# Five columns spread by repeated transposes, an opening in another order, and a last output chunk in two halves of 128 tokens

## The chip, the core and the metric

One core of a Trainium2 chip runs the whole kernel. Its engines work side by side, each in its own program order: TensorE (PE, with its weight loads shown apart as PEld), VectorE (DVE), ScalarE (ACT), GpSimd (POOL) and SyncE (SP), whose queue issues most DMAs; ACT issues some. They wait for each other by semaphores. The metric is the device time of one execution in microseconds, the median of several runs.

## The reference

Two layers over 512 tokens of width 1024, with a context of 256 tokens. Per layer, `h = rmsnorm(x) * (1 + s) + sh`, where shift and scale are columns of `silu(c) @ w_mod + b_mod`. Layer 0 mixes by chunked gMLP spatial gating and by neighbourhood attention (8 heads of 64, window 8 x 16, plus the context keys); layer 1 by a Conformer convolution (31 taps, LayerNorm, SiLU). Each is followed by a squared-ReLU MLP of width 4096. The output is the RMS-normed stream:

```
x = x + g1 * mixer(modulate(rmsnorm(x, g), sh1, s1))
x = x + g2 * (relu(modulate(rmsnorm(x, g'), sh2, s2) @ w1) ** 2 @ w2)
...
return rmsnorm(x, final_g)
```

## The kernel before

Activations lie with the model width on the 128 partitions (8 tiles of 128 x 512 tokens). Each product of 128 x 128 weights by 512 tokens is made of three matmuls in fp32r (`hi*hi`, `lo*hi`, `hi*lo`, lines 88 to 90 in `mm3`), with weights and activations split into a high and a low part: ACT copies the high part (L148 for weights), DVE or POOL subtracts it for the low part (L143). The order of every engine's instructions is written out by hand; nothing is rescheduled.

Statistics of a token are a column: after a matmul against ones with the tokens as stationary side, 128 tokens lie on the partitions. To use them on tiles that have tokens along the free axis, the column has to be repeated and turned. Before, this is a full fp32 matmul, the column broadcast to 128 columns as the stationary side and the identity as the moving side. This is done in five places:

- `deviations` (L441): four columns of the first RMS norm; `silu_rows` (L446): here the eight columns of `silu(c)` are first multiplied into diagonals on DVE (L434), and ones against a diagonal gives the repeated row.
- `weigh` (L963): for each of four pairs of heads, the reciprocals of the softmax sums of the pair's eight blocks, as matmuls of 64 columns each.
- `stats` (L1434): mean and reciprocal deviation of the convolution's LayerNorm, in two calls for each half of the tokens.
- `tail1` (L1581): the last RMS norm's factor for the second half of the tokens.

Opening. `mod_products(f)` makes a quarter of the first modulation in four steps: four matmuls (L457), four more and an ACT copy to `ms` (L462), four transposes (L466), and three small DVE operations that end in `gsA` (L471 to L474). The code between the steps orders the rest: `deviations`, `scaled` (DVE, L498), `silu_rows`, `W.piece` (L148 and L143 for a quarter of a weight tile), `first_operand` (ACT makes the high part of two tiles, L504; DVE the rest, L505, L506) and `first_products` (L493).

Attention. A loop takes the 16 units (pair of heads, quarter of the tokens) two at a time: `scores` for both (PE), `weigh` for the two before (PE, L955), `soften` (DVE L922, ACT exponent L926), and then seven steps n = 0 to 6, each with one `more(1)`: a piece of other work from `filling()` (projections, the spatial gate L790 to L869, and products), in whose staged parts ACT and DVE answer each other. At n = 2 and 3 `turn` transposes the exponents (L939) and ACT copies them (L941); with the last quarter of a pair it takes the reciprocal of the sums (L934). At n = 0, 2, 5 (from the seventh loop round on only at 5) `work(1)` runs one DVE job of the later modulations (L599). After the eighth round the last two `weigh` follow, and PE goes on with `more(100)`.

Tail. `tail1` computes the last 128 rows of the output for the second 256 tokens: matmuls, `evac` (DVE, L1073), square (ACT, L343), sums against ones (L1575), root (L1577), reciprocal (L1578), spread (L1581), copy (L1583), six products on DVE and two on POOL (L1586), four output DMAs on SP (L1588).

Of the kernel before, what the change touches and what calls it, by code (L numbers as in the profile page):

```python
# [17 lines left out]
P = 128  # L18
# [37 lines left out]
def body(ctx: ExitStack, tc: tile.TileContext, I: dict, out: bass.AP):  # L56
# [28 lines left out]


# [345 lines left out]
    dgs = [slot(s="dgc") for _ in range(2)]  # L432
    for k in range(KC):
        dve.tensor_scalar(dgs[k // 4][:, k % 4 * P : k % 4 * P + P], ident, sc[:, k, 0:1], None, op0=ALU.mult)  # L434
    r0 = slot(s="rstd")

    def deviations():

        ps = bank()
        for n in range(4):  # L440
            pe.matmul(ps[:, n * P : (n + 1) * P], dev[:, n : n + 1].to_broadcast([P, P]), ident, start=True, stop=True)  # L441
        act.copy(r0, ps)

    def silu_rows(i):
        ps = bank()
        pe.matmul(ps, ones, dgs[i], start=True, stop=True)  # L446
        return ps
# [52 lines left out]
    def first_operand(f):  # L500
        for k in (2 * f, 2 * f + 1):
            gs, sh = colA(0, k)
            hi, lo = h[k]
            act.activation(hi, x0[k], AF.Identity, scale=gs, bias=sh)  # L504
            dve.tensor_scalar(x0[k], x0[k], gs, sh, op0=ALU.mult, op1=ALU.add)  # L505
            dve.tensor_tensor(lo, x0[k], hi.bitcast(F32), op=ALU.subtract)  # L506
# [6 lines left out]
    next(pm)  # L513
    pbs = [silu_rows(0)]
# [4 lines left out]
    W.piece(0, 0)  # L519
# [371 lines left out]
    sm, pts, po, yb, tot = {}, {}, {}, {}, {}  # L891
# [38 lines left out]
    def turn(u):  # L930
        pts[u] = []
        p_, j = units[u]
        if j == 3:
            dve.reciprocal(tot[p_], tot[p_])  # L934
        for e in range(2):
            s = sm[u][e]
            pt = bank()
            for i in range(4):
                pe.transpose(pt[:, i * P : (i + 1) * P], s[:, i * P : (i + 1) * P], ident)  # L939
            t = blk(s="pt") if u % 2 else mp.tile([P, 512], F32, tag="pt", name=nm("pt"), bufs=2)  # L940
            act.copy(t, pt)  # L941
            pts[u].append(t)
        del sm[u]

    def weigh(u):
# [12 lines left out]
        if j == 3:  # L958

            pr = bank()  # L960
            for i in range(4):
                for e in range(2):
                    pe.matmul(pr[64 * e : 64 * e + 64, i * P : (i + 1) * P],  # L963
                              tot[p_][:, 4 * e + i : 4 * e + i + 1].to_broadcast([P, 64]), ident,
                              start=True, stop=True)
            rs = slot(s="rs")
            act.copy(rs, pr)
            b = ahalf("yb", p_)
            dve.tensor_tensor(tok(b), perm(po[p_]), perm(rs), op=ALU.mult)
            yb[p_] = b  # L970
# [47 lines left out]
    for u in range(0, NU, 2):  # L1018
# [7 lines left out]
        for n in range(7):  # L1026
# [3 lines left out]
            if n == 3:  # L1030
                turn(u + 1)
            if n in ((0, 2, 5) if u < 12 else (5,)):
# [38 lines left out]
    def residual(gate, ss):  # L1071
        def evac(m, ps, t0, t1):
            dve.scalar_tensor_tensor(x[:, m, t0:t1], ps, gate[:, m : m + 1], x[:, m, t0:t1],  # L1073
                                     op0=ALU.mult, op1=ALU.add)
            if ss is not None:
# [284 lines left out]
    def conv_module(h):  # L1360
# [69 lines left out]
        def stats(t0, n):  # L1430

            q, r, ps = stat[t0]
            for i in (2 * n, 2 * n + 1):
                pe.matmul(ps[:, i * P : (i + 1) * P], q[:, i : i + 1].to_broadcast([P, P]), ident,  # L1434
                          start=True, stop=True)
# [96 lines left out]
    def tail1(acts, ev, ss, ff, third):  # L1532
# [35 lines left out]
        seven = together([(7, v, P)], acts, ev, b0, b1)[0]  # L1568
        seven()
        gained((7,))  # L1570
        sq, ss.late = ss.late[0], None
        tot_ = bank()
        for n in range(2):
            for i, t in enumerate((ss.acc[:, b0:b1], sq)):
                pe.matmul(tot_[:, n : n + 1], t[:, n * P : n * P + P], ones[:, :1], start=i == 0, stop=i == 1)  # L1575
# [4 lines left out]
        for n in range(2):  # L1580
            pe.matmul(pr[:, n * P : n * P + P], q[:, n : n + 1].to_broadcast([P, P]), ident, start=True, stop=True)  # L1581
# [5 lines left out]
        for k0, k1 in ((0, 1), (1, 3), (3, 6), (6, 8)):  # L1587
            sync.dma_start(out[:, k0:k1, b0:b1], ob[:, k0:k1, :])  # L1588
# [87 lines left out]
```

## Time and profile before

| what | value |
|---|---|
| median of 3 runs | 1166.35 us (1165.97 to 1166.97) |
| the profiled execution's own time | 1164.55 us |
| its span, first to last instruction | 1162.8 us |
| PE busy, by the modelled ends of its matmuls | 1150.3 us |
| DVE, ACT, POOL busy | 724.8, 479.7, 153.0 us |
| HBM read, written | 152.52 MB, 2.10 MB |

Matmuls overlap in the pipeline, so PE's busy time hides short waits; the distance from one start to the next tells what a matmul costs. An fp32 matmul leaves two records, a transpose or an fp32r matmul one.

### The profile page before, as it was taken

The numbers are of one execution on the slowest core, as the hardware profiler recorded it, in microseconds if no ns is written. First come the engines' busy times: TensorE is split into PE (matmuls) and PEld (weight loads), VectorE is DVE, ScalarE is ACT, GpSimd is POOL, SyncE is SP. The second block draws the span as 40 slices with busy tenths as digits, with TensorE's granted clock in tenths as the row PEclk, the third lists the DMA queues.
The fourth block names the chain that finished last, engine by engine and source line by source line (L and its number), as shares of the span: only waits on it lengthen the run. The fifth ranks groups of instructions, "written<-read, shape, count | busy, mean of one in ns | idle before, by whom it ended". The sixth has DMA issues, their size and how long they took to land. (4 is left out here: it accounts for less than half of the span.)

```text
span 1162.8 us, 16541 instructions
## 1 busy us (share of the span) xinstructions
PE 1150.3 (99%) x6612; PEld 956.9 (82%) x6612; DVE 724.8 (62%) x1258; ACT 479.7 (41%) x955; POOL 153.0 (13%) x149
## 2 busy tenths in 40 slices
PE   9999999999999999999999999999999999999997
PEld 5788898889888888888889666699888888888887
DVE  4855786878665665666677879577643443443544
ACT  5564557446422422423246223575531331332423
POOL 0041234433000000000024110153100000000001
PEclk9999999999999999999999999999999999999998
DMA  9634543351565555555531444313232232232222
GB/s 370 247 125 134 167 149 110 121 192 62 205 236 181 188 210 181 191 207 181 203 123 56 145 126 125 98 37 110 73 109 100 82 109 102 79 109 78 105 73 73
DMA packets 32333, 161.91 MB, mean 139 GB/s; under 512 B 4416, under 2 KB 8000, under 8 KB 16256
## 3 DMA queue, kind: packets, MB, share of 16 engines
q1 hardware_dynamic: 28224, 146.43, 36.5%
q10 hardware_dynamic: 4032, 14.42, 3.6%
q8 instruction: 52, 0.85, 0.3%
q14 instruction: 25, 0.20, 0.1%
HBM read 152.52 MB, written 2.10 MB: 133 GB/s over the span
## 5 line engine op out<-in xcount | busy, mean ns | idle before, releaser
L148 ACT CAST whi<-raw 128x512 fp32r<-128x512 f32 x340 | 191.5, 616 | 196.4 <-PE ps L90 171.9
L88 PE MATMUL ps<-hhi,whi 128*128 128x512 f32 x608 | 238.5, 392 | 0.0
L89 PE MATMUL ps<-hhi,wlo 128*128 128x512 f32 x608 | 236.8, 389 | 0.0
L90 PE MATMUL ps<-hlo,whi 128*128 128x512 f32 x608 | 236.8, 389 | 0.0
L143 DVE TENSOR_TENSOR wlo<-raw,whi 128x512 fp32r<-128x512 f32 x293 | 200.3, 721 | 37.1 <-ACT whi L148 36.3
L90 PE MATMUL ps<-hid,whi 128*128 128x512 f32 (+1 forms) x520 | 196.5, 378 | 0.0
L89 PE MATMUL ps<-hid,wlo 128*128 128x512 f32 (+1 forms) x520 | 196.5, 378 | 0.0
L88 PE MATMUL ps<-hid,whi 128*128 128x512 f32 (+1 forms) x520 | 196.4, 378 | 0.0
L1073 DVE SCALAR_TENSOR_TENSOR x<-ps,mod,x 128x512 f32<-128x512 f32 (+1 forms) x94 | 62.7, 669 | 147.5 <-PE ps L90 142.6
L88 PEld LDWEIGHTS ps<-hhi,whi 128*128 128x128 f32 x608 | 114.2, 188 | 26.6 <-issue 3.2
L90 PEld LDWEIGHTS ps<-hlo,whi 128*128 128x128 f32 x608 | 114.1, 188 | 23.9
L89 PEld LDWEIGHTS ps<-hhi,wlo 128*128 128x128 f32 x608 | 114.2, 188 | 23.0
L143 POOL TENSOR_TENSOR wlo<-raw,whi 128x512 fp32r<-128x512 f32 x47 | 70.0, 1503 | 416.9 <-DVE mod L599 306.8
L599 DVE CUSTOM_DVE_ANT_0 graw<-graw,cB,vec 128x1024 f32<-128x1024 f32 x80 | 109.0, 1364 | 20.8 <-DMA graw<-in_wmB_dram 20.8
L89 PEld LDWEIGHTS ps<-hid,wlo 128*128 128x128 f32 x520 | 97.9, 188 | 18.2
L88 PEld LDWEIGHTS ps<-hid,whi 128*128 128x128 f32 x520 | 97.8, 188 | 18.2
L90 PEld LDWEIGHTS ps<-hid,whi 128*128 128x128 f32 x520 | 97.9, 188 | 17.9
L1209 DVE TENSOR_TENSOR z<-z 128x512 f32<-128x512 f32 (+1 forms) x72 | 46.8, 656 | 90.8 <-ACT z L1207 90.7
L1207 ACT ACTIVATE z<-ps 128x512 f32<-128x512 f32 (+1 forms) x72 | 38.9, 549 | 131.5 <-PE ps L90 129.3
L1213 DVE TENSOR_TENSOR hid<-z,hid 128x512 fp32r<-128x512 f32 (+1 forms) x72 | 45.7, 641 | 43.3 <-ACT hid L1211 43.3
L1211 ACT CAST hid<-z 128x512 fp32r<-128x512 f32 (+1 forms) x72 | 40.6, 572 | 60.6 <-DVE z L1209 60.6
L343 ACT ACTIVATE sq<-x 128x256 f32<-128x256 f32 (+1 forms) x41 | 20.3, 496 | 66.4 <-DVE x L1073 66.3
(271 smaller groups left out, 1712.3 us busy)
## 6 DMA issues: line engine op xcount, KB each, us to landing
raw<-in_w_ff_dram SPq DMA_DIRECT2D x64, 1024.0 KB
graw<-in_wmB_dram SPq DMA_DIRECT2D x28, 1024.0 KB
graw<-in_wmB_dram ACTq DMA_DIRECT2D x24, 512.0 KB
raw<-in_w_pw_dram SPq DMA_DIRECT2D x12, 1024.0 KB
raw<-in_w_in_dram SPq DMA_DIRECT2D x8, 1024.0 KB
wmA<-in_wmA_dram SPq DMA_DIRECT2D x7, 1024.0 KB
y<-ypad SPq DMA_DIRECT2D x90, 67.5 KB
raw<-in_w_out_dram SPq DMA_DIRECT2D x4, 1024.0 KB
```

Of the source, the lines that this page charges most:

```text
L88: pe.matmul(ps, w[0], a[0], start=first, stop=False)
L89: pe.matmul(ps, w[1], a[0], start=False, stop=False)
L90: pe.matmul(ps, w[0], a[1], start=False, stop=last)
L143: (e or dve).tensor_tensor(lo.parts[q], src, hi.parts[q].bitcast(F32), op=ALU.subtract)
L148: act.copy(hi.parts[q], src)
L343: act.activation(sq, src, AF.Square)
L599: dve.tensor_tensor_reduce(out=wv, in0=wv, in1=cB, scale=1.0, scalar=vcol(V_BMOD, l * 48 + q * 8 + j % 8), op0=ALU.mult, op1=ALU.add, accu ...
L1073: dve.scalar_tensor_tensor(x[:, m, t0:t1], ps, gate[:, m : m + 1], x[:, m, t0:t1], op0=ALU.mult, op1=ALU.add)
L1207: act.activation(z, ps, AF.Relu)
L1209: dve.tensor_tensor(z, z, z, op=ALU.mult)
L1211: act.copy(hi, z)
L1213: dve.tensor_tensor(lo, z, hi.bitcast(F32), op=ALU.subtract)
```

## The change

A helper `spread` transposes the column, repeated along the free axis, against the identity. It takes the place of the matmuls in the first, second, fourth and fifth place above; the diagonals on DVE are gone. In the attention the sums' reciprocals are no longer taken in `turn` but in a new `repeat_sums`, which the loop calls at n = 5 of a pair's second round: DVE takes the reciprocal and copies it, repeated 64 times, into 128 x 512 elements of a tile of exponents that has been transposed by then; `weigh` transposes its four blocks of 128. In the opening the weight piece's low part (`lowpiece`) moves into `first_operand`, and the first high part is made by ACT and DVE, half each. In the tail the last chunk's evacuation, square and sum run in two halves of 128 tokens, the sums of the earlier rows come first, and ACT issues the third of the four output DMAs.

```diff
@@ -83,6 +83,10 @@
 
     HALVES = [(0, H), (H, T)]
 
+
+    def spread(ps, col):
+
+        pe.transpose(ps, col.to_broadcast([P, P]), ident)
 
     def mm3(ps, w, a, first, last):
         pe.matmul(ps, w[0], a[0], start=first, stop=False)
@@ -429,21 +433,19 @@
     dve.reciprocal(dev, dev)
 
     cB = cp.tile([P, D], F32, name="cB")
-    dgs = [slot(s="dgc") for _ in range(2)]
-    for k in range(KC):
-        dve.tensor_scalar(dgs[k // 4][:, k % 4 * P : k % 4 * P + P], ident, sc[:, k, 0:1], None, op0=ALU.mult)
     r0 = slot(s="rstd")
 
     def deviations():
 
         ps = bank()
         for n in range(4):
-            pe.matmul(ps[:, n * P : (n + 1) * P], dev[:, n : n + 1].to_broadcast([P, P]), ident, start=True, stop=True)
+            spread(ps[:, n * P : (n + 1) * P], dev[:, n : n + 1])
         act.copy(r0, ps)
 
     def silu_rows(i):
         ps = bank()
-        pe.matmul(ps, ones, dgs[i], start=True, stop=True)
+        for k in range(4):
+            spread(ps[:, k * P : (k + 1) * P], sc[:, 4 * i + k, 0:1])
         return ps
 
 
@@ -501,7 +503,11 @@
         for k in (2 * f, 2 * f + 1):
             gs, sh = colA(0, k)
             hi, lo = h[k]
-            act.activation(hi, x0[k], AF.Identity, scale=gs, bias=sh)
+            t1 = T if k else H
+            act.activation(hi[:, :t1], x0[k][:, :t1], AF.Identity, scale=gs, bias=sh)
+            if t1 < T:
+                dve.tensor_scalar(hi[:, t1:], x0[k][:, t1:], gs, sh, op0=ALU.mult, op1=ALU.add)
+                lowpiece()
             dve.tensor_scalar(x0[k], x0[k], gs, sh, op0=ALU.mult, op1=ALU.add)
             dve.tensor_tensor(lo, x0[k], hi.bitcast(F32), op=ALU.subtract)
 
@@ -511,12 +517,12 @@
     deviations()
     scaled(0)
     next(pm)
+    lowpiece = W.piece(0, 0, late=True)
     pbs = [silu_rows(0)]
     next(pm)
     pbs.append(silu_rows(1))
     keep_warm(1, 256)
     run(pm)
-    W.piece(0, 0)
     wqk = {0: W.his[0]}
     first_operand(0)
     first_products((0, 1), (0, 1), ("hh", "lh"))
@@ -888,7 +894,7 @@
 
 
     units = [(p_, j) for p_ in range(4) for j in range(4)]
-    sm, pts, po, yb, tot = {}, {}, {}, {}, {}
+    sm, pts, po, yb, tot, repeated = {}, {}, {}, {}, {}, {}
 
     def scores(u):
 
@@ -930,8 +936,6 @@
     def turn(u):
         pts[u] = []
         p_, j = units[u]
-        if j == 3:
-            dve.reciprocal(tot[p_], tot[p_])
         for e in range(2):
             s = sm[u][e]
             pt = bank()
@@ -940,7 +944,16 @@
             t = blk(s="pt") if u % 2 else mp.tile([P, 512], F32, tag="pt", name=nm("pt"), bufs=2)
             act.copy(t, pt)
             pts[u].append(t)
+        if j == 3:
+            repeated[p_] = sm[u][1]
         del sm[u]
+
+    def repeat_sums(p_):
+
+        t = tot.pop(p_)
+        dve.reciprocal(t, t)
+        dve.tensor_copy(repeated[p_].rearrange("p (i e d) -> p i e d", e=2, d=64),
+                        t.rearrange("p (e i) -> p i e", i=4).unsqueeze(3).to_broadcast([P, 4, 2, 64]))
 
     def weigh(u):
         p_, j = units[u]
@@ -958,11 +971,9 @@
         if j == 3:
 
             pr = bank()
+            r = repeated.pop(p_)
             for i in range(4):
-                for e in range(2):
-                    pe.matmul(pr[64 * e : 64 * e + 64, i * P : (i + 1) * P],
-                              tot[p_][:, 4 * e + i : 4 * e + i + 1].to_broadcast([P, 64]), ident,
-                              start=True, stop=True)
+                pe.transpose(pr[:, i * P : (i + 1) * P], r[:, i * P : (i + 1) * P], ident)
             rs = slot(s="rs")
             act.copy(rs, pr)
             b = ahalf("yb", p_)
@@ -1029,6 +1040,8 @@
                 turn(u)
             if n == 3:
                 turn(u + 1)
+            if n == 5 and j == 2:
+                repeat_sums(p_)
             if n in ((0, 2, 5) if u < 12 else (5,)):
                 work(1)
             if n == 3 and p_ < 3:
@@ -1069,10 +1082,12 @@
         sync.dma_start(x[:, 4 * i : 4 * i + 4, :], I["xT"][:, 4 * i : 4 * i + 4, :])
 
     def residual(gate, ss):
-        def evac(m, ps, t0, t1):
+        def evac(m, ps, t0, t1, sq=None):
             dve.scalar_tensor_tensor(x[:, m, t0:t1], ps, gate[:, m : m + 1], x[:, m, t0:t1],
                                      op0=ALU.mult, op1=ALU.add)
-            if ss is not None:
+            if sq is not None:
+                act.activation(sq, x[:, m, t0:t1], AF.Square)
+            elif ss is not None:
                 ss.add(x[:, m, t0:t1], t0, t1)
         return evac
 
@@ -1431,8 +1446,7 @@
 
             q, r, ps = stat[t0]
             for i in (2 * n, 2 * n + 1):
-                pe.matmul(ps[:, i * P : (i + 1) * P], q[:, i : i + 1].to_broadcast([P, P]), ident,
-                          start=True, stop=True)
+                spread(ps[:, i * P : (i + 1) * P], q[:, i : i + 1])
             act.copy(r[:, n * H : n * H + H], ps[:, n * H : n * H + H])
 
         def normed(t0, t1):
@@ -1565,27 +1579,31 @@
         sync.dma_start(out[:, 6:8, a0:a1], oa[:, 6:8, :])
         gained((6,))
         ss.flush()
-        seven = together([(7, v, P)], acts, ev, b0, b1)[0]
-        seven()
-        gained((7,))
-        sq, ss.late = ss.late[0], None
+        last = []
+        together([(7, v, P)], acts, lambda m, ps, t0, t1: last.append(ps), b0, b1)[0]()
+        sq = slot(cols=H, s="sq")
         tot_ = bank()
         for n in range(2):
-            for i, t in enumerate((ss.acc[:, b0:b1], sq)):
-                pe.matmul(tot_[:, n : n + 1], t[:, n * P : n * P + P], ones[:, :1], start=i == 0, stop=i == 1)
+            pe.matmul(tot_[:, n : n + 1], ss.acc[:, b0 + n * P : b0 + n * P + P], ones[:, :1],
+                      start=n == 0, stop=False, skip_group_check=True)
+        for n in range(2):
+            t = slice(n * P, n * P + P)
+            ev(7, last[0][:, t], b0 + n * P, b0 + n * P + P, sq[:, t])
+            pe.matmul(tot_[:, n : n + 1], sq[:, t], ones[:, :1], start=False, stop=True, skip_group_check=True)
+        gained((7,))
         q = small(2, "q")
         act.activation(q, tot_[:, :2], AF.Sqrt, bias=epsc, scale=1.0 / D)
         dve.reciprocal(q, q)
         pr = bank()[:, :H]
         for n in range(2):
-            pe.matmul(pr[:, n * P : n * P + P], q[:, n : n + 1].to_broadcast([P, P]), ident, start=True, stop=True)
+            spread(pr[:, n * P : n * P + P], q[:, n : n + 1])
         r = slot(cols=H, s="rstd")
         act.copy(r, pr)
         for e, ks in ((dve, (0, 1)), (pool, (2,)), (dve, (3, 4)), (pool, (5,)), (dve, (6, 7))):
             for k in ks:
                 e.tensor_tensor(ob[:, k, :], ob[:, k, :], pr if e is dve else r, op=ALU.mult)
         for k0, k1 in ((0, 1), (1, 3), (3, 6), (6, 8)):
-            sync.dma_start(out[:, k0:k1, b0:b1], ob[:, k0:k1, :])
+            (act if k0 == 3 else sync).dma_start(out[:, k0:k1, b0:b1], ob[:, k0:k1, :])
         ff.close()
 
     mlp(1, lead1, 0, tail1)
```

## Rows read from the trace of the kernel before

**Rows 1.** The page: busy time of each engine, and the granted TensorE clock in 40 slices of the span, in tenths of full speed.

```profile
PE 1150.3 (99%) x6612; PEld 956.9 (82%) x6612; DVE 724.8 (62%) x1258; ACT 479.7 (41%) x955; POOL 153.0 (13%) x149
...
PEclk9999999999999999999999999999999999999998
```

**Rows 2.** The view of the waits of PE over the whole span: who waited for whom, microseconds in all, times, the longest.

```profile
PE ps L1434 <- DVE zc L1444: 0.5, 1, 0.5
...
PE ps L955 <- ACT pt L941: 0.4, 1, 0.4
...
PE ps L963 <- ACT gelu L824: 0.3, 1, 0.3
```

**Rows 3.** The timeline of PE in the opening: start, length to the last end, line, operands, count of records.

```profile
13.72 1.16 PE L441 MATMUL ps<-kon,dev 128*128 128x128 f32 x8
14.81 1.07 PE L457 MATMUL ps<-wmA,sc 128*32 128x512 f32 x8
15.81 1.12 PE L446 MATMUL ps<-dgc,ones 128*128 128x512 f32 x2
16.77 0.60 PE L466 MATMUL ps<-kon,ms 128*128 128x128 f32 x4
17.20 1.02 PE L446 MATMUL ps<-dgc,ones 128*128 128x512 f32 x2
...
18.90 1.44 PE L493 MATMUL ps<-hhi,whi 128*128 128x512 f32 x4 [0.24 <-ACT hhi L504]
```

**Rows 4.** The timelines of ACT (two rows) and of DVE (one row) in the opening.

```profile
15.94 0.58 ACT L462 COPY ms<-ps 128x512 f32<-128x512 f32 x1 [0.44 <-PE ps L457]
...
18.04 1.52 ACT L504 ACTIVATE hhi<-x,modA,gsA 128x512 fp32r<-128x512 f32 x2 [0.99 <-DVE gsA L474]
...
17.92 0.69 DVE L143 TENSOR_TENSOR wlo<-raw,whi 128x512 fp32r<-128x512 f32 x1
```

**Rows 5.** The view of stretches, for the first 14.3 us: busy time and records of PE, PEld, DVE, ACT, POOL, clock, share and rate of the DMA engines.

```profile
0.00:14.30 14.30, 13.31 (x57) 7.63 (x58) 3.94 (x11) 7.72 (x13) 0.49 (x7) 1.00 0.88 334
```

**Rows 6.** The timeline of PE at the end of the first pair of heads.

```profile
105.72 1.04 PE L963 MATMUL ps<-kon,tot 128*64 128x128 f32 x16
106.69 0.50 PE L88 MATMUL ps<-hhi,whi 128*128 128x512 f32 x1
```

**Rows 7.** The timelines of DVE (two rows) and PE (two rows) at the end of the third pair.

```profile
170.96 0.17 DVE L841 TENSOR_SCALAR gsd<-gmv 128x8 f32<-128x8 f32 x1
171.04 1.28 DVE L599 CUSTOM_DVE_ANT_0 graw<-graw,cB,vec 128x1024 f32<-128x1024 f32 x1
...
170.44 1.09 PE L963 MATMUL ps<-kon,tot 128*64 128x128 f32 x16 [0.26 <-ACT gelu L824]
171.87 0.39 PE L814 MATMUL ps<-whi,hhi 128*128 128x256 f32 x1 [0.34 <-ACT vtok L703]
```

**Rows 8.** The timelines of ACT (one row), DVE (three rows) and PE (two rows) at the end of the fourth pair.

```profile
199.58 0.60 ACT L790 ACTIVATE gelu<-ps 128x512 f32<-128x512 f32 x1
...
198.57 0.19 DVE L934 RECIPROCAL tot<-tot 128x8 f32<-128x8 f32 x1
...
202.31 0.69 DVE L878 SCALAR_TENSOR_TENSOR sg<-sg,u 128x512 f32<-128x512 f32 x1
202.92 1.28 DVE L599 CUSTOM_DVE_ANT_0 graw<-graw,cB,vec 128x1024 f32<-128x1024 f32 x1
...
200.56 1.14 PE L963 MATMUL ps<-kon,tot 128*64 128x128 f32 x15
201.63 0.50 PE L88 MATMUL ps<-hhi,whi 128*128 128x512 f32 x1
```

**Rows 9.** Two lines of the kernel over the whole span: least, median and greatest duration in ns, first and last start.

```profile
L93 DVE CAST kh<-kt x4: 412/418/429, 62.2 to 144.1; 128x512 fp32r<-128x512 f32 x4
...
L143 DVE TENSOR_TENSOR wlo<-raw,whi x293: 675/684/2016, 17.9 to 1134.8; 128x512 fp32r<-128x512 f32 x147
```

**Rows 10.** The timeline of PE in the convolution's LayerNorm.

```profile
745.85 0.71 PE L1434 MATMUL ps<-kon,q 128*128 128x128 f32 x4
746.49 1.50 PE L1334 MATMUL ps<-y,cB 128*32 128x256 f32 x24
```

**Rows 11.** The timelines of PE (three rows), DVE and ACT in the tail.

```profile
1154.08 0.38 PE L1575 MATMUL ps<-ones,sq 128*128 128x1 f32 x2 [0.60 <-ACT sq L343]
...
1154.55 0.36 PE L1575 MATMUL ps<-ones,sq 128*128 128x1 f32 x2
1155.46 0.71 PE L1581 MATMUL ps<-kon,q 128*128 128x128 f32 x4 [0.55 <-DVE q L1578]
...
1153.04 0.48 DVE L1073 SCALAR_TENSOR_TENSOR x<-ps,mod,x 128x256 f32<-128x256 f32 x1
...
1153.61 0.42 ACT L343 ACTIVATE sq<-x 128x256 f32<-128x256 f32 x1 [0.63 <-DVE x L1073]
```

**Rows 12.** The DMA engines from 1157 to 1162 us, busy tenths in 40 slices.

```profile
DMA  0000000199848999999999999899999994000000
```

**Rows 13.** The view of stretches of the tail (columns as in rows 5), and the timeline of PE at the start.

```profile
1152.90:1156.30 3.40, 2.02 (x13) 1.56 (x12) 0.78 (x3) 1.20 (x5) 0.00 (x0) 1.00 0.49 166
1156.30:1162.80 6.50, 0.00 (x0) 0.00 (x0) 2.07 (x6) 0.34 (x1) 1.41 (x2) 0.50 0.49 161
...
0.99 7.04 PE L406 MATMUL ps<-ones 128*128 128x512 f32 x10 [0.99 <-POOL expo L314]
```

## The prediction

> **What bounds the kernel now.** I read the page first: PE is busy 1150.3 of 1162.8 us, and the granted clock stands at its full level in all slices but the last [rows 1]. Then the waits of PE over the whole span: a dozen, none longer than 1 us; three of them lie in stages that the change touches [rows 2]. So the end is set by the number and length of PE's matmuls, and whatever shortens PE's program shortens the time, as long as PE is the one that is waited for. A busy PE does not prove that, since its ends are modelled. So for each of the five places I read the timeline of PE by its starts (the distance from one start to the next is what a matmul costs), and then those of the engines that feed it. Two stages turn out not to be PE's: the end of the attention, where ACT and DVE answer each other and PE waits for them [rows 2, 7, 8], and the tail, a chain through all engines [rows 11].
>
> **The price of a spread.** Eight records for four columns reach from 13.72 to 14.81, 1.09 us; four transposes reach from 16.77 to 17.20, 0.43 us [rows 3]. The first matmul behind an empty weight buffer costs about 0.1 more in either form, so a spread of four columns gains 0.45 us, and one of two columns 0.22.
>
> **Opening.** The path runs from PE's spread through L457, the copy to `ms` and the transposes to `gsA`, ACT's first high part and the first product at 18.90 [rows 3, 4]. The spread is 0.46 shorter, so the second half of L457 begins at 14.35 instead of 14.81. It needs its weight: the stretch to 14.3 us moved 14.3 x 334 = 4.78 MB [rows 5], and the loads up to this one are by the shapes in the code 4.4 MB, so it is there, if only just. The copy to `ms` then runs from 15.48 to 16.07 instead of from 15.94 [rows 4]; the four transposes for `silu(c)`, 0.43, fit before its end. The transposes of `ms` begin at 16.13 instead of 16.77; they now wait for ACT and not for the 0.96 of L446, which costs 0.1 at their first one: 0.54 gained. ACT's first high part is halved: two take 1.52, so one takes some 0.8, and half of one between 0.4 and 0.8, taken as 0.53 since an instruction has a fixed part: another 0.27. Sum 0.81, for the second tile too, which begins earlier by the halving. DVE's eight diagonals go, and they were on nobody's path. DVE's half of the high part comes first and the low part (0.69) after it [rows 4]; the products that read it start four matmuls later, so the move costs nothing; without that cover it would cost about 0.3. From there to the attention PE is not starved, so the 0.8 stays. Ends: 0.3 (the halving alone) and 1.0.
>
> **Attention, first and second pair.** PE's sixteen records reach from 105.72 to 106.69, 0.97 us [rows 6]. They run two at a time on halves of the array, so they were cheap already. Four transposes need 0.43 and about 0.1 for the change of shape: 0.4 gained for each pair, 0.8 for both. DVE has idle time there; the repeated rows are ready some 3 us before they are read.
>
> **Attention, third and fourth pair.** Here the place of `repeat_sums` decides. DVE works in order, and at n = 5 the call stands behind what `more(1)` gave it and ahead of L599. Its price: a small reciprocal with the dependence behind it, 0.2, and a copy of 128 x 512 fp32. The trace has no copy with a repeated source; a plain copy of this size takes 0.42, a subtraction of two tiles 0.68 [rows 9]. I take 0.42, since it is the same operation; both ends go into the range. So 0.6 in all.
> Third pair: the call stands between L841 at 170.96 and L599 at 171.04 [rows 7]. PE would read the rows from 170.44 and gets them at 171.65: PE's own gain is gone, and everything that DVE has behind it is 0.6 later. From there to the fourth pair DVE and ACT run as a chain, the one idle only while the other works, and PE waits for its last copies [rows 2], so these 0.6 go through.
> Fourth pair: the reciprocal stood at 198.57, 2 us before PE read it at 200.56. Now it stands behind L878, that is at 202.92, where L599 began [rows 8]. With the 0.6 from before, and 0.6 of its own, the rows are ready at 204.1. PE, which is done with the work ahead of them at about 200.5, stands still. Four transposes and the change of shape follow, 0.6, so L88 begins at 204.7 instead of 201.63: 3.1 lost, the third pair's part among them. Nothing later gives it back, since PE waits for nobody for long after this. Ends: 2.2 (the third pair's 0.6 absorbed, the copy short) and 3.7 (a long copy twice).
>
> **Convolution.** Four calls of two columns each: the first reaches from 745.85 to 746.49 [rows 10]. Each saves 0.22; one of them waits for DVE [rows 2], but that DVE work hangs on the call before it, which is earlier too. Sum 0.85, ends 0.4 (the waiting one and its forerunner gain nothing) and 0.9.
>
> **Tail.** From 1153.04 to the square's end it takes 0.99, and then PE sums four records up to 1154.91 [rows 11]. In halves: two evacuations of 128 tokens between 0.24 and 0.48, taken as 0.36, then one square between 0.21 and 0.42, taken as 0.31, and 0.1 between engines: PE's last pair begins at 1154.2 and ends 0.38 later, at 1154.58: 0.33 gained. The last spread of 0.71 loses two records of 0.11: 0.22. ACT's scaling of the last rows stays behind the squares and ends before the root. The fourth DMA did not wait for the third: the DMA engines are full from the first bytes to the last [rows 12], so another queue for the third moves nothing. Sum 0.55, ends 0.2 and 0.8.
>
> **The sum.** -0.81 - 0.8 + 3.1 - 0.85 - 0.55 = +0.1. The profiled execution took 1164.55, its span 1162.8; the median of the runs is 1.8 above it, and I add the sum to the median: 1166.4, no change. A difference under 0.2%, 2.3 us, is about what a measurement of this kernel cannot tell from none.
>
> **Rivals.**
> Slower, by the clock after the stall: PE stands still for some 3 us at the fourth pair. In the tail 13 short records in 3.4 us were followed by a fall from 2.4 to 1.2 GHz [rows 13]; the longest waits in the middle of the kernel, 0.5, were not. If the stall is followed by such a fall, the dense products after 204 begin at half the clock. The price by the ten records at the start, 7.04 for what takes 1.02 for two of the shape later [rows 3, 13]: between 1.9 (5 x 1.02 against 7.04) and half of 7.04, 3.5; I take 2.6. That gives 1169.0. Against it: PE is full before and after. It decides with the stall itself: without one there is no fall, and no row shows a stall of this size in the middle of the kernel.
> Slower, by the clock in the opening: between 15.4 and 18.1 PE would have twelve transposes and only the short warming matmuls; before, four long records of L446 stood there [rows 3]. If transposes do not hold the clock, it falls before the first products, for the same 2.6: 1169.0. The trace has no stretch that is mostly transposes. The Trainium skill ("TensorE: Matmul & The Clock Gate", Part 4: PE-mode transpose) says just this, that transposes do not count as busy for the full clock in the way matmuls do; no run here shows it yet.
> Faster: the rows of the third and fourth pair are ready in time, because ACT and DVE are less late there than in this execution. Then both pairs gain 0.4 each and nothing is lost: -0.81 - 1.6 - 0.85 - 0.55 = -3.8, 1162.5. For it: their lateness partly comes from DMAs and from POOL beside DVE, which may fall otherwise. Against it: at the fourth pair DVE would have to be over 3 us earlier.
> The change does not do what it says: a transpose of a repeated column takes the two records of a matmul. Then the halved high part and the halves of the tail remain, 0.6, against 3.5 (the 3.1 of the fourth pair, and 0.4 more since its spread is no shorter): 1169.2. Against it: L466 and L939 transpose fp32 in one.
>
> **Chances.** My forecast 0.55, the clock after the stall 0.18, the clock in the opening 0.10, rows in time 0.11, a spread as dear as before 0.06. My forecast's own range, with the ends of its terms not all on one side, is 1165.2 to 1168.0. The range reaches over the three slower cases and leaves out the fastest: 1164.0 to 1169.3. Over 0.2% faster: the rows in time and a little of the forecast, 0.13; over 0.2% slower lies above 1168.7, two thirds of the three slower cases, 0.23; within 0.2%: 0.64.
>
> **What would show it.** Right: the first L493 near 18.1; L963's place with four records, PE idle before the fourth pair's for about 3 us with DVE's copy as the releaser, L88 behind it at about 203 after the earlier gains; first sum matmuls of the tail before the last evacuation. Wrong: no wait at the fourth pair, or a clock below full anywhere before the end; a copy over 0.7; a first L493 later than 18.6.

## The result, and the profile after

The median went from 1165.68 us (21 runs, 1164.39 to 1167.03) to 1167.51 us (21 runs, 1165.77 to 1169.67): a ratio of 1.0017, with a 95% interval of 1.0011 to 1.0024. That is 1.8 us slower, a little under what I had called no change, and 1.1 above the forecast of 1166.4; the forecast started from a median of 1166.35, so in the difference (+0.1) it is off by 1.7. The profiled execution of after took 1167.51 with a span of 1165.7, 2.9 above the span of before, whose profiled execution was 1.1 under its median here: the two profiles differ by more than the medians do. The changed kernel's lines have moved: the L88, L89 and L90 of before are L92, L93 and L94, L493 is L495, L599 is L605, L939 is L943, L963 is L976, L1334 is L1349, and most spreads now stand under L89.

The page's line of PE, to be read beside [rows 1]: 58 records and 2.9 us of work less, and yet the span is longer.

```profile
PE 1147.4 (98%) x6554; PEld 953.5 (82%) x6554; DVE 732.2 (63%) x1256; ACT 479.4 (41%) x956; POOL 151.3 (13%) x149
```

The waits of PE over the whole span (who waited for whom, us in all, times, the longest), beside [rows 2]: three waits of about 2 us stand in the attention, where none of before was over 0.4.

```profile
PE ps L943 <- ACT s L932: 2.4, 1, 2.4
PE ps L976 <- DVE s L955: 2.3, 1, 2.3
PE ps L976 <- ACT vtok L709: 1.7, 1, 1.7
PE ps L361 <- DVE acc L355: 1.5, 2, 1.0
```

Where the time went is read from the starts of the same matmul in both profiles. The timeline of PE after, at the opening, the ends of the first, third and fourth pair, the convolution's LayerNorm and the tail:

```profile
14.18 0.65 PE L89 MATMUL ps<-kon,dev 128*128 128x128 f32 x4
14.76 1.06 PE L459 MATMUL ps<-wmA,sc 128*32 128x512 f32 x8
...
18.51 0.50 PE L495 MATMUL ps<-hhi,whi 128*128 128x512 f32 x1 [0.45 <-ACT hhi L507]
...
106.00 0.66 PE L976 MATMUL ps<-kon,s 128*128 128x128 f32 x4
106.41 0.48 PE L92 MATMUL ps<-hhi,whi 128*128 128x512 f32 x1
...
171.46 0.36 PE L820 MATMUL ps<-whi,hhi 128*128 128x256 f32 x1
...
205.48 0.63 PE L976 MATMUL ps<-kon,s 128*128 128x128 f32 x4 [2.35 <-DVE s L955]
205.87 0.47 PE L92 MATMUL ps<-hhi,whi 128*128 128x512 f32 x1
...
750.15 0.43 PE L89 MATMUL ps<-kon,q 128*128 128x128 f32 x2
750.52 0.85 PE L1349 MATMUL ps<-y,cB 128*32 128x256 f32 x12
...
1157.51 0.61 PE L1592 MATMUL ps<-ones,sq 128*128 128x1 f32 x4
1158.66 0.43 PE L89 MATMUL ps<-kon,q 128*128 128x128 f32 x2 [0.55 <-DVE q L1596]
```

Against [rows 3, 6, 7, 8, 10, 11], after is 0.39 earlier at the first product (18.51 for 18.90), 0.28 earlier behind the first pair (106.41 for 106.69), 0.41 earlier behind the third (171.46 for 171.87), and then 4.24 later behind the fourth (205.87 for 201.63). It is 5.81 later near 264, still 4.03 later at 750.52, and 3.20 at the last spread. So most of the loss lies between 171 and 206, the one stage of the five whose sum was forecast as a loss.

How that stage lost more than forecast is seen on DVE and POOL. The timelines of DVE (five rows) and POOL (three rows) of after:

```profile
170.50 0.43 DVE L955 COPY s<-tot 128x512 f32<-128x512 f32 x1
170.84 1.28 DVE L605 CUSTOM_DVE_ANT_0 graw<-graw,cB,vec 128x1024 f32<-128x1024 f32 x1
...
172.05 1.51 DVE L797 SCALAR_TENSOR_TENSOR gelu<-gelu 128x256 f32<-128x256 f32 x1
...
180.35 3.61 DVE L800 SCALAR_TENSOR_TENSOR gn<-gelu 128x256 f32<-128x256 f32 x1 [0.49 <-ACT gelu L799]
...
204.91 0.43 DVE L955 COPY s<-tot 128x512 f32<-128x512 f32 x1
...
170.38 1.64 POOL L848 TENSOR_TENSOR gsd<-gsd,expo 128x8 f32<-128x8 f32 x1 [7.67 <-DVE gsd L847]
171.98 1.30 POOL L147 TENSOR_TENSOR wlo<-raw,whi 128x512 fp32r<-128x512 f32 x1
...
179.91 3.77 POOL L147 TENSOR_TENSOR wlo<-raw,whi 128x512 fp32r<-128x512 f32 x3
```

The copy took 0.43, as I had taken it. But L797 at 172.05 and L800 at 180.35, products of two tiles that mostly take 0.42, took 1.51 and 3.61. Each began while a low part of POOL's (L147) was running, and L800 ended 0.28 after the third of three such parts.

And the clock fell. The view of stretches of after (busy time and records of PE, PEld, DVE, ACT, POOL, granted clock, share and rate of the DMA engines): behind the wait of 2.4 us at L943 stands a stretch at half the clock, 1.2 for 2.4 GHz, and the second stall, from 203, has none behind it.

```profile
190.00:194.50 4.50, 2.08 (x14) 1.34 (x13) 4.49 (x13) 2.54 (x7) 1.67 (x1) 1.00 0.01 2
194.50:198.00 3.50, 3.50 (x14) 3.00 (x13) 0.00 (x0) 3.50 (x11) 0.00 (x0) 0.51 0.44 150
...
203.00:205.50 2.50, 0.15 (x5) 0.05 (x1) 2.40 (x6) 0.31 (x1) 0.00 (x0) 1.00 0.64 265
205.50:211.00 5.50, 5.50 (x27) 4.60 (x28) 2.30 (x4) 0.59 (x1) 0.00 (x0) 1.00 0.28 98
```

### The profile page after: what moved, and what is told of

It is laid out like the page before. It is cut to its first block, busy times and chain, and to the rows that moved or that the text cites. A ratio compares the mean times of both kernels' runs of the same rounds, so it can differ in the third digit from the quotient of the medians.

```text
span 1165.7 us, 16431 instructions
## 1 busy us (share of the span) xinstructions
PE 1147.4 (98%) x6554; PEld 953.5 (82%) x6554; DVE 732.2 (63%) x1256; ACT 479.4 (41%) x956; POOL 151.3 (13%) x149
## 4 chain that ended last, share of the span: by engine, by line
PE 86%; DVE 6%; ACT 3%; DMA 2%; issue 1%; POOL 1%; DVEq 0%; ACTq 0%; POOLq 0%
PE ps L92 22%; PE ps L93 22%; PE ps L94 22%; PE ps L1349 3%; PE ps L225 3%; PE ps L228 3%; PE ps L226 3%; PE ps L495 2%; DMA raw<-in_w_ff_dram 1%; ACT s L932 1%; DVE gn L800 1%; PE ps L410 1%; PE ps L915 1%; PE ps L459 1%; PE ps L968 1%
## 5 line engine op out<-in xcount | busy, mean ns | idle before, releaser
L152 ACT CAST whi<-raw 128x512 fp32r<-128x512 f32 x340 | 191.6, 616 | 197.7 <-PE ps L94 171.8
L92 PE MATMUL ps<-hhi,whi 128*128 128x512 f32 x608 | 238.6, 393 | 0.0
L94 PE MATMUL ps<-hlo,whi 128*128 128x512 f32 x608 | 237.1, 390 | 0.0
L93 PE MATMUL ps<-hhi,wlo 128*128 128x512 f32 x608 | 236.9, 390 | 0.0
L147 DVE TENSOR_TENSOR wlo<-raw,whi 128x512 fp32r<-128x512 f32 x293 | 200.5, 721 | 38.6 <-ACT whi L152 37.7
L94 PE MATMUL ps<-hid,whi 128*128 128x512 f32 (+1 forms) x520 | 196.3, 378 | 0.0
L93 PE MATMUL ps<-hid,wlo 128*128 128x512 f32 (+1 forms) x520 | 196.3, 378 | 0.0
L92 PE MATMUL ps<-hid,whi 128*128 128x512 f32 (+1 forms) x520 | 196.3, 378 | 0.0
L1086 DVE SCALAR_TENSOR_TENSOR x<-ps,mod,x 128x512 f32<-128x512 f32 (+2 forms) x95 | 62.8, 664 | 147.2 <-PE ps L94 142.4
L92 PEld LDWEIGHTS ps<-hhi,whi 128*128 128x128 f32 x608 | 114.4, 188 | 26.1 <-issue 3.0
L94 PEld LDWEIGHTS ps<-hlo,whi 128*128 128x128 f32 x608 | 114.3, 188 | 24.0
L93 PEld LDWEIGHTS ps<-hhi,wlo 128*128 128x128 f32 x608 | 114.4, 188 | 22.9
L147 POOL TENSOR_TENSOR wlo<-raw,whi 128x512 fp32r<-128x512 f32 x47 | 69.0, 1481 | 418.4 <-DVE mod L605 306.8
L605 DVE CUSTOM_DVE_ANT_0 graw<-graw,cB,vec 128x1024 f32<-128x1024 f32 x80 | 107.6, 1346 | 21.2 <-DMA graw<-in_wmB_dram 21.2
L92 PEld LDWEIGHTS ps<-hid,whi 128*128 128x128 f32 x520 | 97.9, 188 | 18.2
L94 PEld LDWEIGHTS ps<-hid,whi 128*128 128x128 f32 x520 | 97.9, 188 | 18.1
L93 PEld LDWEIGHTS ps<-hid,wlo 128*128 128x128 f32 x520 | 97.9, 188 | 18.0
```

Of the source, the lines that this page charges most:

```text
L92: pe.matmul(ps, w[0], a[0], start=first, stop=False)
L93: pe.matmul(ps, w[1], a[0], start=False, stop=False)
L94: pe.matmul(ps, w[0], a[1], start=False, stop=last)
L147: (e or dve).tensor_tensor(lo.parts[q], src, hi.parts[q].bitcast(F32), op=ALU.subtract)
L152: act.copy(hi.parts[q], src)
L605: dve.tensor_tensor_reduce(out=wv, in0=wv, in1=cB, scale=1.0, scalar=vcol(V_BMOD, l * 48 + q * 8 + j % 8), op0=ALU.mult, op1=ALU.add, accu ...
```

## The experiments

The twelve kernels were run in three lots, each beside the kernel before on the same chip; differences are of medians against the before of the lot (1165.58, 1165.40 and 1165.71). By the intervals of the ratios a difference is good to about 1 us where the kernel ran eleven times and to 1.5 us where it ran five times (the attention's part alone, the early copies, two pairs only, the short copy); a difference between two of the kernels is good to about 2 us. Each kernel has one profile, of one execution.

**The attention's part taken away.** The changed kernel with the reciprocal back in the second turn and the sixteen matmuls back at L976; `repeat_sums` is gone.

> The changed kernel with the attention's spread of the sums as it was before (sixteen matmuls, the reciprocal at the turn); the four other places stay changed. Theory A (the whole loss comes from repeat_sums standing late in DVE's order, so that PE waits at the third and fourth pair): what is left is the opening, the convolution and the tail, about 2.0 us faster than the kernel before, and no wait of PE over 1 us between 165 and 207. Rival B (the loss is mostly a chance meeting of DVE with POOL's low parts near 180, which any shift of DVE's program can bring): no faster than the kernel before by more than 0.5, and the long DVE instruction near 180 is still there.

Measured: 1163.61, 2.0 faster than before, ratio 0.9979 (0.9970 to 0.9988). No wait of PE over 0.4 between 165 and 207. Theory A (that it fits to the tenth is chance); of B, the long instruction near 180 is not there.

**The attention's part alone,** on the kernel before.

> The kernel before with the attention's part of the change alone. Theory A: about 3.9 us slower than the kernel before (the changed kernel's 1.8 and the 2.0 that the other places give). Rival B: within 1 us of the changed kernel's own difference, so 0.8 to 2.8 slower, since the other places give little and the meeting with POOL falls as it likes.

Measured: 1169.34, 3.8 slower, 1.0033 (1.0020 to 1.0045). Theory A. The waits are those of after (2.4 and 1.7, and 2.9 in place of 2.3 for DVE's copy), and the two long DVE instructions take 1.51 and 3.63.

**The same copies, earlier.** One call moved:

```
             if n == 3:
                 turn(u + 1)
+                if j == 2:
+                    repeat_sums(p_)
...
-            if n == 5 and j == 2:
-                repeat_sums(p_)
```

> The changed kernel with repeat_sums called at n = 3, right behind the second turn, where the reciprocal stood before, and not at n = 5. Theory A: the rows are ready before PE reads them in all four pairs, no wait at L976 over 0.5 us, and the time is 2.5 to 3.5 us under the kernel before. Rival (the copy into the score tile then waits for PE's transposes of that tile, and DVE's queue behind it too; or the meeting with POOL remains): PE still waits for DVE in the fourth pair, and the time is within 1 us of the kernel before.

Measured: 1160.99, 4.6 faster than before, 0.9963 (0.9951 to 0.9976). That beats both kernels, and goes further than theory A said. PE has no wait for DVE at L976; the longest there is 0.8, for ACT. The timelines of DVE (three rows), POOL (three rows) and PE (two rows) of this run:

```profile
170.32 1.28 DVE L605 CUSTOM_DVE_ANT_0 graw<-graw,cB,vec 128x1024 f32<-128x1024 f32 x1
...
171.53 0.42 DVE L797 SCALAR_TENSOR_TENSOR gelu<-gelu 128x256 f32<-128x256 f32 x1
...
198.16 0.43 DVE L955 COPY s<-tot 128x512 f32<-128x512 f32 x1
...
170.49 2.60 POOL L848 TENSOR_TENSOR gsd<-gsd,expo 128x8 f32<-128x8 f32 x1 [8.30 <-DVE gsd L847]
173.06 1.30 POOL L147 TENSOR_TENSOR wlo<-raw,whi 128x512 fp32r<-128x512 f32 x1
...
180.80 4.22 POOL L147 TENSOR_TENSOR wlo<-raw,whi 128x512 fp32r<-128x512 f32 x3
...
200.05 0.66 PE L976 MATMUL ps<-kon,s 128*128 128x128 f32 x4
200.46 0.48 PE L92 MATMUL ps<-hhi,whi 128*128 128x512 f32 x1
```

The copy of the fourth pair lies at 198.16, where DVE had nothing to do, and is read at 200.05. At 170 the order is turned round: DVE's L605 begins 0.17 before POOL's power (L848, 128 x 8), which then takes 2.60 in place of 1.64, so that POOL's low part begins only at 173.06, and L797 is through by then.

**Transposes for two pairs only.** The first two pairs as changed, the last two as before.

> The changed kernel in which only the first two pairs take the transposes, and the last two the sixteen matmuls with the reciprocal at the turn. Theory A: the first two pairs give 0.4 each on top of the run with the old sums, so about 2.8 us under the kernel before. Rival B: as the run with the old sums, within 0.3, or slower than it, since the two copies on DVE cost as much as PE saves.

Measured: 1161.10, 4.5 faster, 0.9962 (0.9950 to 0.9975): faster than theory A by 1.7, and level with the early copies. The first two pairs are worth 0.48 each in its profile, as in after (below); what else came is told at the end.

**The opening alone,** on the kernel before.

> The kernel before with the opening's part of the change alone. Theory A (the forecast's term): 0.8 us faster, the first L495 some 0.8 earlier against the moment at which the chain starts, and that lead still there at 106. Rival B (what the opening gains is lost again at 40, where ACT and PE wait for the context rows that a DMA brings at its own time): within 0.3 us of the kernel before.

Measured: 1165.29, 0.1 faster, 0.9999 (0.9990 to 1.0007). The interval reaches from 1.2 faster to 0.8 slower, so it leaves the forecast's 0.8 just inside and decides little. In its profile the lead of 0.3 at the first product (18.59) is still there at 104; rival B's loss at 40 is not seen in this run. Near 240 the profile falls 0.2 behind before.

**The convolution and the tail alone.**

> The kernel before with the convolution's and the tail's part of the change alone. Theory A (the forecast's terms): 0.85 and 0.55, so 1.4 us faster than the kernel before. Rival B (one wait for DVE's zc in the convolution takes what its four spreads give, and in the tail the full DMA engines do): 0.5 us or less.

Measured: 1164.32, 1.1 faster, 0.9987 (0.9978 to 0.9995). Between the two theories, nearer to A.

**Late in the third pair only:** the run with the early copies, with the third pair's call at n = 5.

```
-                if j == 2:
+                if j == 2 and u != 10:
                     repeat_sums(p_)
+            if n == 5 and u == 10:
+                repeat_sums(p_)
```

> The run with the early sums, but with repeat_sums at n = 5 in the third pair only (u = 10); the fourth pair's stays early. Theory A, as the forecast had it (the 0.6 us of DVE's small reciprocal and copy pass through the chain of ACT and DVE): PE waits 0.6 longer than in the run with the early sums, about 0.6 us over its time, near 1161.6. Rival B (the shift lets DVE's gelu near 172 and 180 begin inside POOL's low parts, as in the changed kernel, and DVE stands there 1.1 and 3.2 us): the scores of the fourth pair are softened 1.7 us later, PE waits over 2 us at L943 near 192, and the time is 1.5 to 2.5 us over the run with the early sums, near 1163.

Measured: 1163.29, 2.1 faster than before, so 2.5 over the early copies. Rival B. L797 took 1.51 at 172.02, L800 took 3.62 at 180.33, PE waited 2.4 at L943, and the clock stood at half from 194.0 to 197.5. The profiled execution is one of the longer ones (1165.28).

**Late in the fourth pair only** (the same with u = 14).

> The run with the early sums, but with repeat_sums at n = 5 in the fourth pair only (u = 14). Theory A: no DVE instruction of 1.5 or 3.6 us near 172 and 180; the rows of the fourth pair are ready some 0.6 after DVE's L884, PE stands still about 2.8 us at L976 near 200, and the time is 2.5 to 3 us over the run with the early sums, near 1163.8. Rival B (the stall is mostly the collision's lateness, which is not there now): under 1.5 us over the run with the early sums.

Measured: 1165.76, 0.4 over before and 5.0 over the early copies: more than theory A. One of theory A's signs failed, for near 181 DVE met POOL here too, if more mildly: L797 took 1.47 and L800, at 183.12, took 0.94. Up to there the program is that of the early copies. The timelines of DVE (two rows), POOL and PE of this run, and then one stretch of it (columns as above):

```profile
170.76 1.28 DVE L605 CUSTOM_DVE_ANT_0 graw<-graw,cB,vec 128x1024 f32<-128x1024 f32 x1
...
181.17 1.47 DVE L797 SCALAR_TENSOR_TENSOR gelu<-gelu 128x256 f32<-128x256 f32 x1 [0.32 <-ACT gelu L796]
...
170.71 1.64 POOL L848 TENSOR_TENSOR gsd<-gsd,expo 128x8 f32<-128x8 f32 x1 [8.31 <-DVE gsd L847]
...
203.42 0.63 PE L976 MATMUL ps<-kon,s 128*128 128x128 f32 x4 [2.90 <-DVE s L955]
203.81 0.48 PE L92 MATMUL ps<-hhi,whi 128*128 128x512 f32 x1
...
204.90 0.63 PE L92 MATMUL ps<-hhi,whi 128*128 128x512 f32 x1
205.33 0.63 PE L93 MATMUL ps<-hhi,wlo 128*128 128x512 f32 x1
```

```profile
204.00:207.60 3.60, 3.60 (x11) 2.77 (x10) 1.74 (x4) 0.59 (x1) 0.00 (x0) 0.53 0.39 146
```

L605 stood 0.14 for a DMA that fills its rows (L590), so POOL's power began 0.06 ahead of it, where with the early copies it began 0.17 behind: the order turned with no edit ahead of it. PE's wait at L943 was 0.5 all the same, and PE had lost 0.2 by 196. L92 begins at 203.81 for 200.46 with the early copies: 3.35, the stall and 0.4 by which this execution was later ahead of it. Then the same products follow at 0.43 from start to start, where 0.23 is usual: the clock is at half up to 207.6. Against the same products of before, PE's lag grows from 2.18 (203.81 for 201.63, [rows 8]) to 3.66 at 207.46: the fall costs 1.5.

**One copy that nobody reads,** in the third pair's place:

```
             repeated[p_] = sm[u][1]
+            dead[p_] = sm[u][0]
...
+            if n == 5 and u == 10:
+                dve.tensor_copy(dead[p_], repeated[p_])
```

> The run with the early sums, and at n = 5 of u = 10, where the third pair's repeat_sums stood, one extra DVE copy of 128 x 512 that nobody reads (its target is a score tile that is done with); 0.34 us of DVE. The output is untouched. Theory A (what counts is the order in which POOL's small power at L848 and DVE's long L605 begin: if the power goes first, POOL's low part at L147 comes some 1.1 us earlier and falls on DVE's chain, there and again near 181): PE waits about 2 us at L943 near 192, and the time is 1.5 to 2.5 us over the run with the early sums, near 1163. Rival (the late rows themselves made the third pair's cost, by PE's wait): 0.4 us or less over it, near 1161.3.

Measured: 1163.70, 2.0 faster than before, 2.6 over the early copies. Theory A: the copy costs about as much as the late call did (2.5) though no one waits for its result. Of its eleven times five lie at or under 1162.82 and six at or above 1163.70, the profiled one among the six, so the meeting that this profile shows need not come in every execution. The timelines of DVE and POOL, and then a wait of PE:

```profile
171.27 1.28 DVE L605 CUSTOM_DVE_ANT_0 graw<-graw,cB,vec 128x1024 f32<-128x1024 f32 x1
...
181.52 3.37 DVE L797 SCALAR_TENSOR_TENSOR gelu<-gelu 128x256 f32<-128x256 f32 x1 [0.29 <-ACT gelu L796]
...
171.10 1.74 POOL L848 TENSOR_TENSOR gsd<-gsd,expo 128x8 f32<-128x8 f32 x1 [8.32 <-DVE gsd L847]
```

```profile
PE ps L943 <- ACT s L932: 1.9, 1, 1.9
```

Of the two meetings only the second came, and it was enough.

**Three such copies.**

> As the run with one copy, with three of them, 1.03 us of DVE. Theory A: POOL's power goes first as well, DVE stands in its low part for a shorter while, so not three times the cost of one copy but about the same or up to 1 us more: 1163 to 1164. Rival (each us of DVE passes through the chain as it is): 1.0 over the run with the early sums, near 1162.

Measured: 1165.64, level with before, 4.5 over the early copies. Both meetings are there (1.51 at 173.33, 3.62 at 181.63), and the 1 us of DVE on top. Both theories had it too cheap: A by 1.6 from its upper end, the rival by 3.6.

**A short copy** of 128 x 128.

> As the run with one copy, with a copy of 128 x 128 in its place, about 0.1 us of DVE: shorter than the 0.17 by which L605 began before POOL's L848 in the run with the early sums. Theory A: L605 still begins first, POOL's power takes 2.6 us as there, DVE has no instruction of 1.5 us near 172, and the time is within 0.4 us of the run with the early sums. Rival (any shift there brings the meeting): as with one copy.

Measured: 1161.42, 4.3 faster than before, 0.3 over the early copies. Theory A. The margin was thin, 0.04 us:

```profile
170.57 1.28 DVE L605 CUSTOM_DVE_ANT_0 graw<-graw,cB,vec 128x1024 f32<-128x1024 f32 x1
...
170.61 2.74 POOL L848 TENSOR_TENSOR gsd<-gsd,expo 128x8 f32<-128x8 f32 x1 [8.31 <-DVE gsd L847]
```

**PE kept at work in the fourth pair's stall:**

```
             r = repeated.pop(p_)
+            if p_ == 3:
+                for _ in range(6):
+                    pe.matmul(pr, ones, ones.unsqueeze(1).to_broadcast([P, 4, P]), start=True, stop=True)
```

> The run with the fourth pair late, with six matmuls of 128 x 512 on ones, 2.6 us of PE, ahead of the fourth pair's transposes and into the same bank, which the transposes then overwrite. Theory A (the stall of 2.9 us is what the clock's fall at 204 follows, and the fall costs 1.5 us): PE works through the stall, the granted clock stays at its full level until the tail, L92 begins near 203.8 as it did, and the time is about 1.5 us under the run with the fourth pair late, near 1164.3. Rival (the clock falls in any case, or its fall costs nothing since the work behind is bound by others): no faster than the run with the fourth pair late, 1165.8 or above.

Measured: 1167.04, 1.3 over the run with the stall. My sizing was wrong: an fp32 matmul is two records, as [rows 3] had shown, so the six took 5.2 us and L92 began only at 206.70. The clock is the part that can be read:

```profile
201.00:206.30 5.30, 5.30 (x14) 2.34 (x13) 4.69 (x9) 0.63 (x1) 0.00 (x0) 1.00 0.41 170
206.30:211.00 4.70, 4.70 (x24) 3.94 (x23) 0.69 (x1) 0.59 (x1) 0.00 (x0) 1.00 0.30 112
```

With PE at work there is no fall. PE's lag behind before is 5.07 at L92 and still 5.04 some 4 us on, where with the stall it grew by 1.5. That this saves 1.5 was not shown as a time, since the filling was too long.

## Why the prediction was right, and where its steps were not

The time lies in the range and on the side of no change, but two terms of the sum were wrong by more than the total. In the table the middle column is my sum, the right one what the profiles of before and after differ by over the same stretch (their sum is 2.9 before rounding).

| Step | Forecast | Between the profiles |
|---|---|---|
| Opening, up to 104 us | -0.81 | +0.2: 0.85 gained, the start 0.46 later, about 0.6 lost by 104 |
| First and second pair | -0.8 | -1.0 |
| Third and fourth pair, to 206 us | +3.1 | +5.0 |
| 206 to 260 us | 0 | +1.6 |
| Around 736 us | 0 | -1.3 |
| Convolution | -0.85 | -0.9 with 0.2 of drift ahead of it |
| Tail | -0.55 | -0.8 |

**Opening.** The mechanism and its size were right. From the spread of `dev` to the first product it is 5.18 in before (13.72 to 18.90, [rows 3]) and 4.33 in after: 0.85 for 0.81. The same 0.84 to 0.86 stands in the ten other profiles with the changed opening. That after began its spread 0.46 later (14.18 for 13.72) is not its doing: the kernel with the old opening that has only the convolution and the tail changed began 0.8 later. "So the 0.8 stays" is not borne out: from the first product to 104 us these profiles lose between nothing (the opening alone) and 0.7 of it, one of them 1.4, mostly near 40. What it is worth in the end stays open within 1 us. The rival that transposes let the clock fall here is refuted for this stretch: in after the clock is at 1.00 from 6.8 to 194.5, the twelve transposes that follow one another from 15.76 to 17.46 included. The Trainium skill ("TensorE: Matmul & The Clock Gate", Part 4: PE-mode transpose) says that a transpose doesn't count as busy in the way a matmul does; with 1.7 us of transposes, and products ahead of and behind them, that rule had no effect to be seen.

**First and second pair.** As forecast: 0.97 became 0.41 at the first (106.00 to 106.41), 0.1 of it given back by the change of shape.

**Third pair: the step that failed first.** "These 0.6 go through" treated DVE's delay as an amount. It was a change of order. In [rows 7] L599 begins 0.08 behind L841; in after the reciprocal and the copy stand between them, POOL's power gets in first; POOL's low part then begins at 171.98 and not, as with the early copies, at 173.06, so 1.1 earlier, while DVE's L797 is 0.5 later, and the two meet. Late in the third pair alone cost 2.5, and a copy that nobody reads 2.6, while one short enough for L605 to stay ahead of POOL cost 0.3: neither the late rows nor the amount of work by itself made the price, but who began first. That is not the whole of it: in the profile of the run with the fourth pair late POOL was first as well, and PE lost only 0.2 by 196. It takes, besides, that DVE's products come while a low part runs, and how long they then take differs (0.94 to 3.63). The Trainium skill ("SBUF — State Buffer", SBUF: two separate sides) says that VectorE, with two inputs in SBUF, and GpSimd hold a port pair against each other for a whole instruction; the trace agrees, with 2.60 for 1.64 on POOL's side and 1.51 for 0.42 on DVE's. That one DVE instruction stood through three of POOL's (3.61) is more than the page says, and in the run with the early copies one got in between two of them (L800 at 181.88, 0.58), as did L797 in the run with the fourth pair late (181.17, 1.47); what decides that was not found. I had named POOL beside DVE only as a reason why the lateness might be less.

**Fourth pair.** Right in its mechanism: L976 waited for DVE's copy, as the prediction's list of signs said. The rows came at 205.3 instead of 204.1, because L884 began 1.75 later than the L878 of [rows 8] (204.07 for 202.31) and not 0.6 later.

**The clock after the stall,** my rival at 0.18, is a part of what happened, though in after it came behind the wait of 2.4 at L943 and not behind the fourth pair's stall, where the rival had it. A clock below full before the end also stood among my signs of being wrong. Over the runs it came behind the stalls of 2.9 (late in the fourth pair; the attention's part alone), and behind the wait of 2.4 or 1.9 at L943 in four profiles (after, late in the third pair, one copy, three copies), but not behind that of 2.4 in a fifth (the attention's part alone), nor behind the 2.3 of after. Its price was 1.5 where dense products stood behind it, under the lowest end that I had given (1.9). In after's profile it was hidden: PE's lag grew to 3.4 us at 198.1 and was 2.3 again at 202.9 (before waits 0.43 for ACT's copies there, after does not), and PE then stood until 205.48 for DVE's copy in any case. The prediction treated this rival and the forecast as alternatives, and they add up. Early copies against both late is 6.4 us (4.6 and 1.8), of which the forecast and its rival "rows in time" had 3.9 (0.1 and 3.8).

**From 206 to 260 us** 1.6 more was lost: 0.3 near 240, which the run with only the convolution and the tail changed loses too, and 1.3 with a longer wait (1.0) at L361 for DVE's sums. That wait stands in three of the four profiles in which DVE met POOL both near 172 and near 181 (after, late in the third pair, three copies; not the attention's part alone, which loses 0.3 there) and in no other; the chain between them was not followed, and the prediction's "nothing later gives it back" had no thought for a further loss.

**Convolution and tail.** A spread of two columns and what follows is 0.37 from start to start (750.15 to 750.52) for 0.64 in [rows 10], 0.27 saved for the 0.22 forecast; 0.3 of the four was given back at 769. In the tail the way from the last evacuation to the spread went from 2.42 ([rows 11], 1153.04 to 1155.46) to 1.96 (1156.70 to 1158.66). The third DMA on ACT's queue moved nothing, as argued: the DMA engines are full from the first bytes to the last in after as in [rows 12].

**What made the sum look right** was luck: a gain of 1.3 that I had not foreseen near 736 us, and 0.2 more in the tail, paid for much of the third pair.

## What to carry to other kernels

Where a change adds an instruction to an engine that takes turns with another, ask not only how long it is but whose instruction it lets begin first: 0.34 us of DVE cost 2.6 us here, and 0.14 us cost 0.3, each good to about 2 us. A margin of 0.17 us in such an order can be lost to a DMA that comes a little later, so one profile doesn't settle it. A value that an idle moment of the engine could have made is worth placing by the timeline, since the same copies at n = 3 in place of n = 5 turned 1.8 us lost into 4.6 gained. A stall of PE is priced with its length and with the products behind it at half the clock.

## What the runs showed that I had not expected

In before, the convolution's matmuls, four at a time on quarters of the array, are broken up near 736: two records at 735.77, the next at 736.55, with 0.19 put down to "issue", and about 1.3 us lost by 737 against after. The runs with the old attention have it too, as the waits and the page's DMA queues show for the run with the opening alone:

```profile
PE ps L1342 <- issue: 0.4, 1, 0.4
```

```profile
PE 1149.5 (99%) x6612; PEld 956.2 (82%) x6612; DVE 723.2 (62%) x1251; ACT 479.5 (41%) x955; POOL 153.4 (13%) x149
...
q8 instruction: 52, 0.85, 0.3%
```

None with the attention's new spreads has it, even in two pairs only. It goes with the number of PE's records, 6602 and 6612 with it and 6554 to 6578 without, and with 52 packets in the queue that brings instructions, for 51 in every profile without. That suggests the loading of PE's program, but it was not tried. It explains 1.3 of the 1.7 by which the kernel with two pairs changed beat its forecast, and about as much for the early copies.

The clock can fall behind less than the waits above: in the run with the short copy it stood at half from 171.8 to 175.2, behind two waits of 0.9 and 0.8, and in the run with the early copies it did not, behind two of 0.8. The time did not show it there, as PE waited for ACT later on.
